# Second branch's keys and queries moved from the token-major stage into the quarter-product stage of a streaming-encoder kernel

## The chip, the cores and the metric

One core of one Trainium2 chip. The time is device microseconds of one launch. The engines are TensorE (PE, with its weight loads PEld), VectorE (DVE), ScalarE (ACT), GpSimd (POOL) and SyncE (SP), which issues most of the DMAs. Each engine works off its own list of instructions in the order of the program; they wait for each other through semaphores.

## The reference

One layer of a hybrid attention trunk, for 1024 prompt tokens and 64 sample tokens (1088 in all), width 1024. What the change touches is the projection of the second branch's queries and keys, and their norm over the 64 channels of each head:

```python
def rms_norm(x, w):
    xf = x.astype(jnp.float32)
    ms = jnp.mean(xf * xf, axis=-1, keepdims=True)
    return (xf * lax.rsqrt(ms + EPS)).astype(x.dtype) * w

def project(x, norm_w, w_in, q_norm_w, k_norm_w):
    h = rms_norm(x, norm_w) @ w_in                      # w_in: 1024 x 6144
    sb_q, sb_k, sb_v, sb_z, cb_q, cb_k, cb_v, cb_z, g_sb, g_cb = jnp.split(h, SPLIT_POINTS, axis=-1)
    ...
    cb_q = rms_norm(cb_q.reshape(lead + (N_HEADS_CB, HEAD_DIM)), q_norm_w)
    cb_k = rms_norm(cb_k.reshape(lead + (N_HEADS_CB, HEAD_DIM)), k_norm_w)
```

`cb_q` and `cb_k` are 512 columns each: 8 heads of 64. Behind them come two attentions (stick-breaking for the first branch, softmax over a band for the second), gates, projections and an output product. The last 512 prompt tokens and the sample tokens of `cb_k` are outputs too. All is float32.

## The kernel before

Every float32 operand of a product is split into a rounded high part and a low part (what rounding left), and a product is three matmuls: high by high, high by low, low by high.

**Token-major stage** (the block that begins at L198; product loop L450 to L537). The input is normed and transposed into `xhl` (channels on the partitions, 1088 tokens along the row). Then eight blocks of 256 columns of `w_in` (the list `NB`, L208) are multiplied, for 9 token tiles each, with tokens on the output's partitions: 8 channel blocks by 3 parts, 24 matmuls of 256 columns to a tile, 16 for the sample tile, 208 for a block. Two blocks are `sb_v`, two `cb_v`; the other four are `cb_k` (2560, 2816) and `cb_q` (2048, 2304). For these four, `evac_nat` copies the tile out and squares it on ACT, sums the squares of each head on DVE, and takes the power -1/2 on POOL (`rsqrt`, L247); `norm_nat` multiplies by it and by the weight on DVE one tile later; `post_nat` transposes the tile on PE (L349), splits it on ACT and DVE, and SP stores it. In the same loop SP loads the next weights, the caches are transposed (`cache_pair`), the bias table is written out (`make_rb`), and from the sixth block on `make_t` makes on DVE and ACT the sums of quarters of the input that the next stage needs (L502 to L515).

**Quarter-product stage** (L544 to L657). The list `pairs` (L145) names 12 pairs of 128-column blocks: keys and queries of the first branch (`k`, `q`), gates `silu` and `sig`. A pair is 256 columns by 1088 tokens, and is computed channel-major (columns of `w_in` on the output's partitions) by seven products of half the channels, 128 columns and half the tokens, with sums and differences of quarters as operands. A product `s` runs in two pieces (`XC`, L29) of 256 and 288 tokens with 12 matmuls each (L634), so a pair is 168 matmuls. Products 0, 1 and 2 open PSUM banks 1, 2 and 3; products 3, 4, 5 and 6 add to banks 1, 2, 2 and 3 (`BANK`, L614). ACT copies product 0 to `s1`; DVE adds after products 1, 4, 5 and 6; a finished quarter goes to `emit`: after product 3, product 4 (`u3`), product 5 (`s1`) and product 6 (`u2`), two pieces each. Product 5 adds to the bank that DVE reads after product 4, so it cannot start before that read.

`emit` applies the gate, or splits the quarter into high and low on ACT and DVE, and hands a store to a list (`soon`, L550) that `step` works off at the start of later products. Keys of the first branch are also transposed back on PE for their output (`out`, L590) through the two banks of `psF`. `prep` and `presum` make the operands of the product five and six places ahead: DVE sums quarters of weights (L401), ACT rounds them (L433), POOL takes the low parts (L434).

The order of all instructions is the order in which the Python code issues them; there is no planner. Behind this stage come the attention with the last projection units as filler (L782 to L1229) and the output product.

Of the kernel before, what the change touches and what calls it, by code (L numbers as in the profile page):

```python
# [8 lines left out]
F32 = mybir.dt.float32  # L9
# [23 lines left out]
def hybrid_step_kernel(ctx: ExitStack, tc: tile.TileContext, x_prompt, x_sample, c_sbk, c_sbv, c_cbk, c_cbv,  # L33
# [114 lines left out]
    for p in (0, 2):  # L148
        pairs += [("silu", 1536 + 128 * p, d_z["sb"][p:p + 2]), ("silu", 3584 + 128 * p, d_z["cb"][p:p + 2])]
# [48 lines left out]
    with ExitStack() as ph:  # L198
        sx = ExitStack()
        natx = sx.enter_context(tc.tile_pool(name="natx", bufs=2))  # L200
        pn = ph.enter_context(tc.tile_pool(name="pn", bufs=2, side="right"))
        p1x = ExitStack()
# [5 lines left out]
        NB = [1024, 2560, 2816, 2048, 2304, 1280, 3072, 3328]  # L208
        nb = len(NB)
        xts, xns, hl, cks = {}, {}, {}, {}  # L210
# [21 lines left out]
        wqk = pn.tile([128, 2, 64], F32, name="wqk", bufs=1)  # L232
# [3 lines left out]
        def load_rb():  # L236
            rbs[0] = p1.tile([128, 8, 257], F32, name="ck", bufs=1)
            SP.dma_start(rbs[0], rel_bias[0:1].to_broadcast([128, 8, 257]))

        def make_rb(h):  # L240
            rb = rbs[0]
            rx = p1.tile([128, 768], F32, name="rx", bufs=3)
# [53 lines left out]
        def evac_nat(i, t, ps):  # L296
# [6 lines left out]
            if grp in (2, 6):  # L303
                v = pn.tile([128, 256], F32, name="vst", bufs=3)
                A.activation(v[:r], ps[:r, :], AF.Copy)
                dst = d_sbv if grp == 2 else d_cbv
                SP.dma_start(dst[t * 128:t * 128 + r, n0:n0 + 256], v[:r])
                if grp == 2:
                    SP.dma_start(tok(o_sbv_p, o_sbv_s, t)[:, n0:n0 + 256], v[:r])
                elif t == 8:  # L310
                    SP.dma_start(o_cbv_s[:, n0:n0 + 256], v[:r])
                elif t >= 4:
                    SP.dma_start(o_cbv_p[(t - 4) * 128:(t - 3) * 128, n0:n0 + 256], v[:r])
                return
            sq = p1.tile([128, 256], F32, name="sqn")
            ms = p1.tile([128, 4], F32, name="msn")
            rs = p1.tile([128, 4], F32, name="rsn", bufs=3)
            qn = p1.tile([128, 4, 64], F32, name="qn", bufs=5)
            A.activation(qn[:r].rearrange("p h d -> p (h d)"), ps[:r, :], AF.Copy)
            A.activation(sq[:r], ps[:r, :], AF.Square)  # L320
            V.tensor_reduce(ms[:r], sq[:r].rearrange("p (h d) -> p h d", d=64), axis=AX.X, op=OP.add)
            rsqrt(rs[:r], ms[:r], 1.0 / 64, 4)
            return qn, rs

        def norm_nat(i, t, qn, rs):
            r = rows(t)
            n0 = NB[i] % 512
            isk = 1 if NB[i] // 512 == 5 else 0
            V.tensor_tensor(out=qn[:r], in0=qn[:r], in1=rs[:r, :, None].to_broadcast([r, 4, 64]), op=OP.mult)
            V.tensor_tensor(out=qn[:r], in0=qn[:r], in1=wqk[:r, None, isk, :].to_broadcast([r, 4, 64]),  # L330
                            op=OP.mult)
            if isk:
                if t == 8:
                    SP.dma_start(o_cbk_s[:, n0:n0 + 256], qn[:r].rearrange("p h d -> p (h d)"))
                elif t >= 4:
                    SP.dma_start(o_cbk_p[(t - 4) * 128:(t - 3) * 128, n0:n0 + 256],
                                 qn[:r].rearrange("p h d -> p (h d)"))

        def post_nat(i, t, qn):
            r = rows(t)  # L340
            c0 = NB[i]
            isk = 1 if c0 // 512 == 5 else 0
            p0 = (c0 % 512) // 128
            if t in (8, 4):
# [1176 lines left out]
```

## Time and profile before

| | us |
|---|---|
| median of 3 runs (lowest, highest) | 988.35 (987.6, 989.67) |
| the profiled execution's own time | 986.78 |
| its span | 985.0 |
| token-major products, from the first to the first quarter product | 227.5 from the start |
| quarter-product stage | 227.5 to 483.1 |
| PE busy | 962.0 |
| DVE, ACT, POOL busy | 630.1, 510.4, 346.2 |

The page of a profile gives busy times; the chain of work says which engine's instructions the end of the kernel hangs on; a table by groups of instructions gives the mean duration of one. A matmul's listed duration (278 ns for 256 columns) is its way through the array: the matmuls overlap, and the cost of one is the distance to the next, which the chain shows as a stretch of many. Idle time of an engine that is not the bottleneck costs nothing.

### The profile page before, as it was taken

What the parts mean: (1) busy time and instruction counts of PE and PEld (TensorE: products, weight loads), DVE (VectorE), ACT (ScalarE), POOL (GpSimd) and SP (SyncE); (2) the same over time, 40 slices, a digit from 0 to 9 for tenths busy, and PEclk for the clock granted to TensorE, in tenths of its full rate; (3) what the DMA queues carried; (4) which work ended last, traced back from release to release, by engine and by line L of the source; (5) the groups of instructions that cost most, each with busy time, mean ns of one, the idle gap of its engine ahead of it and who ended that gap; (6) DMA issues with size and microseconds to landing.
All of it is one profiled execution on the core that took longest, in us unless ns stands there. A gap on an engine that the chain in (4) does not pass through costs nothing.

```text
span 985.0 us, 20439 instructions
## 1 busy us (share of the span) xinstructions
PE 962.0 (98%) x7568; PEld 917.6 (93%) x7568; DVE 630.1 (64%) x1188; ACT 510.4 (52%) x1142; POOL 346.2 (35%) x356
## 2 busy tenths in 40 slices
PE   5999999999999999999999999999999999999998
PEld 5999999999999999999998888898888888999998
DVE  5456665696454655532239898997767765599735
ACT  5534443344443433433248787786876875466220
POOL 3376664115444554444211101101201101486641
PEclk9999999999999999999999999999999999999999
DMA  6727567533656333343298656666898772852642
GB/s 229 223 89 243 193 223 253 166 103 120 180 174 203 115 110 101 99 124 99 79 244 221 172 160 161 164 187 169 232 262 226 213 221 68 264 177 83 210 131 86
DMA packets 174243, 166.97 MB, mean 170 GB/s; under 512 B 34688, under 2 KB 160000, under 8 KB 174016
## 3 DMA queue, kind: packets, MB, share of 16 engines
q1 hardware_dynamic: 165424, 157.34, 53.7%
q10 hardware_dynamic: 8720, 8.33, 2.6%
q8 instruction: 60, 0.98, 0.4%
q14 instruction: 39, 0.32, 0.1%
HBM read 106.89 MB, written 58.72 MB: 168 GB/s over the span
## 4 chain that ended last, share of the span: by engine, by line
PE 90%; DMA 3%; ACT 3%; DVE 1%; SPq 1%; issue 1%; POOL 1%; DVEq 0%; ACTq 0%
PE b L634 25%; PE acc L464 19%; PE b L1435 8%; PE o L1127 7%; PE acc L782 7%; PE z L1033 6%; PE pt L1088 6%; PE b L924 5%; PE acc L882 3%; DMA wrawx<-in_w_in_dram 1%; PE pk L349 1%; ACT wT L1097 1%; PE pt L277 1%; SPq L51 1%; PE acc L1471 1%
## 5 line engine op out<-in xcount | busy, mean ns | idle before, releaser
L122 POOL TENSOR_TENSOR wlo<-wraw,whi 128x1024 fp32r<-128x1024 f32 x22 | 57.6, 2618 | 103.0 <-ACT whi L115 102.9
L1088 PE MATMUL pt<-ident,be 128*128 128x128 f32 (+1 forms) x568 | 87.2, 278 | 5.7 <-ACT wT L1097 1.9
L1056 DVE TENSOR_TENSOR_SCAN kp<-kp,imp 128x128 f32<-128x128 f32 (+7 forms) x64 | 88.3, 1379 | 0.6 <-ACT kp L1036 0.6
L1033 PE MATMUL z<-ks,sq 128*128 128x320 f32 (+5 forms) x384 | 83.2, 325 | 0.0
L1088 PEld LDWEIGHTS pt<-ident,be 128*128 128x128 f32 (+1 forms) x568 | 65.9, 140 | 16.8 <-issue 5.7
L1097 ACT ACTIVATE wT<-pt 128x512 f32<-128x512 f32 (+3 forms) x125 | 58.6, 501 | 39.0 <-PE pt L1088 38.9
L464 PE MATMUL acc<-whi,xa 128*128 128x256 f32 x256 | 74.2, 292 | 0.0
L464 PE MATMUL acc<-wlox,xm 128*128 128x256 f32 x256 | 70.8, 278 | 0.0
L464 PE MATMUL acc<-whi,xm 128*128 128x256 f32 x256 | 70.8, 278 | 0.0
L464 PE MATMUL acc<-wlo,xa 128*128 128x256 f32 x256 | 70.7, 278 | 0.0
L464 PE MATMUL acc<-whix,xb 128*128 128x256 f32 x256 | 70.7, 278 | 0.0
L464 PE MATMUL acc<-whix,xm 128*128 128x256 f32 x256 | 70.6, 278 | 0.0
L1033 PEld LDWEIGHTS z<-ks,sq 128*128 128x128 f32 x384 | 65.8, 188 | 1.1 <-issue 0.2
L1127 PE MATMUL o<-wT,vp 128*64 128x256 f32 (+1 forms) x608 | 66.7, 357 | 0.1
L782 PE MATMUL acc<-xm,whi 128*128 128x384 f32 (+1 forms) x192 | 65.2, 340 | 0.0
L1127 PEld LDWEIGHTS o<-wT,vp 128*64 128x64 f32 x608 | 42.3, 136 | 23.9 <-issue 5.7
L1057 DVE TENSOR_TENSOR be<-be,kp 128x128 f32<-128x128 f32 (+8 forms) x68 | 57.3, 843 | 9.4 <-ACT sg L757 0.5
L1036 ACT ACTIVATE kp<-z 128x384 f32<-128x384 f32 (+6 forms) x104 | 52.4, 504 | 9.5 <-PE z L1033 4.5
L642 DVE TENSOR_TENSOR u<-b,s 128x256 f32<-128x256 f32 (+1 forms) x48 | 20.8, 439 | 56.3 <-PE b L634 55.2
L1037 ACT ACTIVATE be<-z 128x384 f32<-128x384 f32 (+6 forms) x104 | 52.9, 508 | 0.0
L1060 ACT ACTIVATE be<-be,sm 128x640 f32<-128x640 f32 (+5 forms) x68 | 47.2, 694 | 9.5 <-DVE sm L1059 9.2
L1047 ACT ACTIVATE be<-be,sm 128x640 f32<-128x640 f32 (+5 forms) x68 | 47.2, 694 | 3.7 <-DVE sm L1039 3.4
(300 smaller groups left out, 3147.4 us busy)
## 6 DMA issues: line engine op xcount, KB each, us to landing
wraw<-in_w_in_dram SPq DMA_DIRECT2D x32, 512.0 KB, 4.6
wrawx<-in_w_in_dram SPq DMA_DIRECT2D x16, 512.0 KB, 4.5
sq<-d_qsbT SPq DMA_DIRECT2D x32, 192.0 KB, 3.6
sq<-d_qcbT SPq DMA_DIRECT2D x32, 192.0 KB, 4.4
xt<-in_x_prompt_dram SPq DMA_DIRECT2D x8, 512.0 KB, 5.8
d_kcbT<-hl SPq DMA_DIRECT2D x8, 512.0 KB, 4.4
d_qcbT<-hl SPq DMA_DIRECT2D x8, 512.0 KB, 5.7
d_ksbT<-hl SPq DMA_DIRECT2D x16, 256.0 KB, 2.5
```

The lines of the kernel that those rows point to most:

```text
L122: (eng or G).tensor_tensor(out=l, in0=raw, in1=h[:].bitcast(F32), op=OP.subtract)
L464: TE.matmul(ps, x, w, start=m == 0, stop=m == len(steps) - 1)
L634: TE.matmul(ps[:, :m], w[:, hl_, k], right[s](x)[:, k, a:b], start=s < 3 and k == 0 and e == 0, stop=k == 3 and e == 2, skip_group_check=s ...
L782: TE.matmul(ps[:, :b - a], w[:, k], xk(x, k)[:, a:b], start=k == 0 and n == 0, stop=k == KT - 1 and n == 2)
L1033: TE.matmul(z[:, :m], s[:, e, q0:q0 + 128], ks[:, h, o + x:o + y], start=e == parts[0][0], stop=e == parts[-1][0])
L1037: A.activation(be[:r, x:y], z[:r, :m], AF.Sigmoid, scale=0.125)
L1056: V.tensor_tensor_scan(kp[:r, n - 1::-1], kp[:r, n - 1::-1], im[:, ::-1], 0.0, op0=OP.mult, op1=OP.add)
L1057: V.tensor_tensor(out=be[:r, :n], in0=be[:r, :n], in1=kp[:r, 1:n + 1], op=OP.mult)
L1088: TE.transpose(pt[:kr, x, :r], be[:r, kb * 128:kb * 128 + kr], ident[:r, :r])
L1097: A.activation(w[:, sl:sl + m, q0:q0 + r], pt[:, :m, :r], AF.Copy)
L1127: TE.matmul(o[hd * 64:hd * 64 + 64, c0:c1], vv[:kr, kb, hd * 64:hd * 64 + 64], wT[b, p, j, hd, s // 4][:kr, s % 4, c0:c1] if j < 4 else wT ...
L1435: TE.matmul(ps[:, t], left[s](xs_, k)[:, ts_], wt_[:, k], start=s < 3 and t == k == e == 0, stop=k == 3 and e == 2, skip_group_check=s > 2 ...
```

## The change

The four `cb_k` and `cb_q` blocks leave the token-major stage (`NB` has four blocks left), and `norm_nat` and `post_nat` go. The list `pairs` gets two `ck` and two `cq` pairs, each set ahead of one of the four `silu` pairs, so there are 16 pairs. A `ck` or `cq` quarter goes to a new function, `normed`, in four steps that are spread over the following products, so that they run in the pair behind:

- `squares`, three products later: ACT squares the quarter and rounds the square, POOL takes the low part;
- `scale`, between the two pieces of the next product: PE multiplies both parts by `ones`, a block matrix with two 64 by 64 blocks of ones, so that each partition of the result holds the sum over its head; ACT takes the square root, DVE the reciprocal, both in place in a bank of `psF`; DVE multiplies the quarter by it and by the weight `wn`, in one instruction;
- `parts`, at the start of the product after: ACT and DVE split it, and SP stores it one product later;
- `k_out`, two products after `parts`, for the keys whose tokens are outputs: transposes back on PE.

Buffers change with it: `hl` has 8 instead of 4, `s1` and `u2` 4, `u3` 2, `ko` 3; the block of product 3 is one fixed tile (`w3`), and its second buffer holds the squares (`hold`). The bias table and caches move to other pools and earlier places, and `make_t` starts in the second block instead of the sixth.

```diff
@@ -146,7 +146,8 @@
     for p in (0, 2):
-        pairs += [("silu", 1536 + 128 * p, d_z["sb"][p:p + 2]), ("silu", 3584 + 128 * p, d_z["cb"][p:p + 2])]
+        pairs += [("ck", 2560 + 128 * p, p), ("silu", 1536 + 128 * p, d_z["sb"][p:p + 2]),
+                  ("cq", 2048 + 128 * p, p), ("silu", 3584 + 128 * p, d_z["cb"][p:p + 2])]
...
@@ -198,16 +199,22 @@
+        ones = natx.tile([128, 128], F32R, name="ones", bufs=1)
+        wn = natx.tile([128, 2], F32, name="wn", bufs=1)
...
-        NB = [1024, 2560, 2816, 2048, 2304, 1280, 3072, 3328]
+        NB = [1024, 1280, 3072, 3328]
...
+        for h in (slice(0, 64), slice(64, 128)):
+            G.memset(blk2[h, h], 1.0)
...
@@ -495,11 +455,17 @@
-                if (i, ti) == (4, 2):
+                if (i, ti) == (2, 6):
                     load_rb()
-                if 0 <= 9 * i + ti - 40 < 8:
-                    make_rb(9 * i + ti - 40)
-                if i >= 5 and p1x is not None and not pend and not raw1 and ti >= 3:
+                if 0 <= 9 * i + ti - 27 < 8:
+                    make_rb(9 * i + ti - 27)
...
+                if (i, ti) == (1, 1):
                     p1x.close()
...
-                    tw = [3]
+                    tw = [1]
...
@@ -574,10 +536,13 @@
+            p = arg + w
+            if kind in ("ck", "cq"):
+                normed(kind == "ck", p, half, c, n, src, ps)
+                return
...
+        def normed(isk, p, half, c, n, src, ps):
+
+            if ps:
+                kf = up.tile([128, 288], F32, name="kf", bufs=2)
+                V.tensor_copy(kf[:, :n], src[:, :n])
+                src = kf
+            x = src[:, :n]
+            dst = (d_kT if isk else d_qT)["cb"][p]
+
+            def squares():
+                sq = hold[:, 288 * nsq[0]:288 * nsq[0] + n]
+                nsq[0] = (nsq[0] + 1) % 3
+                h = up.tile([128, 2, 288], F32R, name="hl", bufs=HB)
+                A.activation(sq, x, AF.Square)
+                A.activation(h[:, 0, :n], sq, AF.Copy)
+                G.tensor_tensor(out=h[:, 1, :n], in0=sq, in1=h[:, 0, :n].bitcast(F32), op=OP.subtract)
+                mids.append([1, lambda: scale(h)])
+
+            def scale(h):
+                pt = psF.tile([128, 512], F32, name="acc")[:, :n]
+                for e in range(2):
+                    TE.matmul(pt, ones, h[:, e, :n], start=e == 0, stop=e == 1)
+                A.activation(pt, pt, AF.Sqrt, bias=eps64)
+                V.reciprocal(pt, pt)
+                V.scalar_tensor_tensor(x, x, wn[:, 1:2] if isk else wn[:, 0:1], pt, op0=OP.mult, op1=OP.mult)
+                soon(0, parts)
+
+            def parts():
+                h = up.tile([128, 2, 288], F32R, name="hl", bufs=HB)
+                A.activation(h[:, 0, :n], x, AF.Copy)
+                V.tensor_tensor(out=h[:, 1, :n], in0=x, in1=h[:, 0, :n].bitcast(F32), op=OP.subtract)
+                soon(0, lambda: stores(rdma, half, c, h[:, :, :n], dst[:]))
+                if isk and (half or c):
+                    soon(1, lambda: k_out(src, p, half, c, c * 256 if half else None, o_cbk_p, o_cbk_s))
+
+            soon(2, squares)
...
                     m = b - a
+                    if c:
+                        step(mids)
```

How the instructions stand. On DVE, before, in the first `silu` pair of the quarter-product stage (`u` and `s` are quarters, `b` a bank, `ws` a sum of weights, `hl` a result to store), from the adds after product 1 to the quarter after product 4:

```order
L642 TENSOR_TENSOR u_4507<-b_4494,s_4472 128x256
L642 TENSOR_TENSOR u_4522<-b_4509,s_4487 128x288
L401 TENSOR_TENSOR ws<-wraw,wrawx 128x512
L401 TENSOR_TENSOR ws<-ws,wraw 128x512
L574 TENSOR_TENSOR hl<-hl,b_4459 128x256
L574 TENSOR_TENSOR hl<-hl,b_4474 128x288
L642 TENSOR_TENSOR u_4608<-b_4494,s_4472 128x256
L642 TENSOR_TENSOR u_4622<-b_4509,s_4487 128x288
L654 TENSOR_TENSOR u_4608<-b_4531,u_4608 128x256
L574 TENSOR_TENSOR hl<-hl,u_4608 128x256
L654 TENSOR_TENSOR u_4622<-b_4544,u_4622 128x288
L574 TENSOR_TENSOR hl<-hl,u_4622 128x288
```

There a DVE instruction of the pair follows the PE product that feeds it, with weight sums in between. On DVE, after, in the first `silu` pair, which now follows a `ck` pair, from the first add after product 1 (L649 is the add that was L642, L363 the weight sum that was L401; `acc` is a bank of `psF`):

```order
L649 TENSOR_TENSOR u_3244<-b_3231,s_3183 128x256
L597 RECIPROCAL acc<-acc 128x256
L598 SCALAR_TENSOR_TENSOR u_3070<-u_3070,wn,acc 128x256
L597 RECIPROCAL acc<-acc 128x288
L598 SCALAR_TENSOR_TENSOR u_3084<-u_3084,wn,acc 128x288
L649 TENSOR_TENSOR u_3271<-b_3258,s_3210 128x288
L363 TENSOR_TENSOR ws<-wraw 128x512
L363 TENSOR_TENSOR ws<-ws,wraw 128x512
L604 TENSOR_TENSOR hl<-u_3070,hl 128x256
L604 TENSOR_TENSOR hl<-u_3084,hl 128x288
L597 RECIPROCAL acc<-acc 128x256
L598 SCALAR_TENSOR_TENSOR s_2939<-s_2939,wn,acc 128x256
```

The second add of product 1 now stands behind two reciprocals and two multiplications of the pair before. Further on in the same pair, on DVE, from the first gate (L536) to the first add after product 4 (L649):

```order
L536 TENSOR_TENSOR hl<-hl,b_3170 128x256
L597 RECIPROCAL acc<-acc 128x256
L598 SCALAR_TENSOR_TENSOR u_2974<-u_2974,wn,acc 128x256
L597 RECIPROCAL acc<-acc 128x288
L598 SCALAR_TENSOR_TENSOR u_2989<-u_2989,wn,acc 128x288
L536 TENSOR_TENSOR hl<-hl,b_3197 128x288
L604 TENSOR_TENSOR hl<-u_2974,hl 128x256
L604 TENSOR_TENSOR hl<-u_2989,hl 128x288
L649 TENSOR_TENSOR u_3437<-b_3231,s_3183 128x256
```

The add after product 4, which product 5 waits for, has the last group's reciprocals ahead of it. On ACT, before, in the first `silu` pair, around its first gate:

```order
L433 ACTIVATE wlo<-ws 128x512
L572 ACT_TABLE_LOAD
L572 ACTIVATE hl<-b_4459 128x256
L572 ACTIVATE hl<-b_4474 128x288
L433 ACTIVATE whix<-ws 128x512
L572 ACTIVATE hl<-u_4608 128x256
L572 ACTIVATE hl<-u_4622 128x288
```

One load of a function table stands there, and none in the pairs behind. On ACT, after, at the first gate of the first `silu` pair:

```order
L567 ACTIVATE kos<-acc 32x128
L603 ACTIVATE hl<-s_2939 128x256
L603 ACTIVATE hl<-s_2954 128x288
L534 ACT_TABLE_LOAD
L534 ACTIVATE hl<-b_3170 128x256
L596 ACT_TABLE_LOAD
L596 ACTIVATE acc<-acc,eps 128x256
L596 ACTIVATE acc<-acc,eps 128x288
L534 ACT_TABLE_LOAD
L534 ACTIVATE hl<-b_3197 128x288
```

Square roots (L596) and gates (L534) now alternate, with a table load at each turn. With the one ahead of the pair's first square root that is four to each `ck` or `cq` pair, 16 in the whole stage, where one stood before.

More of the change, by code (lines that the diff above doesn't have):

```diff
@@ L315, in evac_nat @@
[L315 to L337, printed above, removed]
@@ L588, in emit, with k_out @@
                 V.tensor_copy(kf[:, :n], src[:, :n])
-            def out():
-                pt = psF.tile([128, 512], F32, name="acc")
-                ko = up.tile([128, 2, 128], F32, name="ko", bufs=4)
-                cols = slice(p * 128, (p + 1) * 128)
+            soon(2 if (w, half) == (0, 1) else 1,
+                 lambda: k_out(kf, p, half, c, half * 512 + c * 256, o_sbk_p, o_sbk_s))
+        def k_out(kf, p, half, c, a, o_p, o_s):
+            pt = psF.tile([128, 512], F32, name="acc")
+            cols = slice(p * 128, (p + 1) * 128)
+            if a is not None:
```

148 lines of the change are left out of this document (64 added, 84 removed).

## The prediction

> **What bounds the kernel now.** I read the page first, then the quarter-product stage in the table by stretches, the chain, the waits of DVE in that stage, and last the durations by shape.
>
> ```profile
> span 985.0 us, 20439 instructions
> PE 962.0 (98%) x7568; PEld 917.6 (93%) x7568; DVE 630.1 (64%) x1188; ACT 510.4 (52%) x1142; POOL 346.2 (35%) x356
> ...
> 172.00:227.00 55.00, 55.00 (x487) 55.00 (x486) 46.47 (x62) 22.56 (x45) 8.76 (x4) 1.00 0.42 132
> 227.50:483.00 255.50, 255.50 (x2058) 254.63 (x2057) 119.20 (x232) 99.54 (x228) 121.42 (x84) 1.00 0.43 129
> ...
> DVE u L642 <- PE b L634: 55.2, 34, 6.8
> ```
>
> PE is busy for 98% of the span. The columns of the two stretches are length, then PE, PEld, DVE, ACT and POOL busy: in the whole quarter-product stage (the second) PE never stops, and DVE and ACT work less than half the time. The last row says who waits: DVE for PE, 55.2 us in 34 waits. So today work on DVE or ACT there costs nothing, and the time is the number of matmuls. The chain prices them:
>
> ```profile
> 168.94 0.22 PE pk L349 x2
> ...
> 172.21 55.33 PE acc L464 x488
> ...
> 256.39 0.44 PE acc L595 x4
> 256.82 0.11 PE acc L597
> ...
> 301.28 181.86 PE b L634 x1464
> ```
>
> A token-major matmul is 55.33/488 = 0.1134 us, a quarter-product matmul 181.86/1464 = 0.1242 us, a transpose 0.11 us.
>
> **PE's own work.** Removed: 4 blocks x 208 x 0.1134 = 94.3 us, and 72 transposes (4 blocks, 9 tiles, 2 each) x 0.11 = 7.9 us: -102.2 us. Added: 4 pairs x 168 x 0.1242 = 83.5 us; the products by ones, 32 quarters' pieces x 2 x 0.1242 = 7.9 us; key transposes, 6 for each of 4 column blocks x 0.11 = 2.6 us: +94.0 us. Net -8.2 us, all on the path, if nothing new makes PE wait.
>
> **What new work runs beside it.** Each `ck` or `cq` pair sends 8 pieces (4 quarters of 256 and 288 tokens) through `normed`, and nearly all of it falls into the first five products of the pair behind. The rows for it, DVE first:
>
> ```profile
> L1059 DVE RECIPROCAL sm<-sm 128x1 f32<-128x1 f32 x68 | 10.5, 154 | 1.9 <-ACT be L1047 1.9
> L537 DVE TENSOR_SCALAR wqk<-wqk 128x64 f32<-128x64 f32 x1 | 0.2, 178 | 0.0
> L244 DVE TENSOR_SCALAR rx<-ck 128x256 f32<-128x256 f32 x8 | 2.3, 283 | 0.0
> L1099 DVE COPY wT<-pt 128x512 f32<-128x512 f32 x21 | 14.5, 689 | 2.2 <-PE pt L1088 2.0
> L1099 DVE COPY wT<-pt 128x128 f32<-128x128 f32 x18 | 5.1, 284 | 0.3 <-PE pt L1088 0.3
> L642 DVE TENSOR_TENSOR u<-b,s 128x288 f32<-128x288 f32 x24 | 10.9, 455 | 20.7 <-PE b L634 20.6
> L642 DVE TENSOR_TENSOR u<-b,s 128x256 f32<-128x256 f32 x24 | 10.1, 422 | 35.6 <-PE b L634 34.6 <-ACT s L638 0.8
> L266 DVE SCALAR_TENSOR_TENSOR xn<-xt,rs,nw 128x512 f32<-128x512 f32 x16 | 11.3, 748 | 5.7 <-POOL rs L249 5.7
> L574 DVE TENSOR_TENSOR hl<-hl,u 128x288 f32<-128x288 f32 x8 | 3.7, 458 | 4.1 <-ACT hl L572 4.1
> L574 DVE TENSOR_TENSOR hl<-hl,u 128x256 f32<-128x256 f32 x8 | 3.4, 426 | 10.1 <-ACT hl L572 10.1
> L401 DVE TENSOR_TENSOR ws<-wraw,wrawx 128x512 f32<-128x512 f32 x4 | 4.2, 1062 | 0.0
> L401 DVE TENSOR_TENSOR ws<-ws,wraw 128x512 f32<-128x512 f32 x8 | 11.4, 1429 | 0.3
> ```
>
> *The reciprocal* decides the size. The trace has it for one column only. Were it like other work from a bank, it would cost what L642 does, 0.42 and 0.46 us: the lower end. But its 154 ns for one column is long: a TENSOR_SCALAR without columns is 178 - 64 x (283 - 178)/192 = 143 ns, a copy from a bank 284 - 128 x (689 - 284)/384 = 149 ns. So its one column takes 5 to 11 ns, where the copy's takes 1.05. I take 7.5 ns a column on 0.15 us, since the RECIPROCAL row is the operation itself: 2.07 us for 256 columns, 2.31 for 288. The upper end is 11 ns: 2.96 and 3.31 us. The Trainium skill, "VectorE: DVE Perf Modes", section "First, the fixed hardware budget", says the reciprocal is an iterated divide with a repeat count of 8. Eight of the copy's columns would be an estimated 8.4 ns, and the sum below about 8 us longer; one column of 5 to 11 ns agrees, but no run here shows a long one.
>
> ACT's rows, then POOL's and SP's:
>
> ```profile
> L572 ACT ACT_TABLE_LOAD x1 | 1.3, 1283 | 0.0
> ...
> L433 ACT ACTIVATE wlo<-ws 128x512 fp32r<-128x512 f32 x24 | 15.1, 630 | 33.3 <-DVE ws L401 30.7 <-PE b L634 2.3
> L572 ACT ACTIVATE hl<-u 128x288 f32<-128x288 f32 x16 | 7.1, 445 | 9.5 <-DVE u L649 5.8 <-DVE u L654 3.5
> L572 ACT ACTIVATE hl<-u 128x256 f32<-128x256 f32 x16 | 6.7, 418 | 35.4 <-DVE u L654 14.0 <-issue 8.6 <-DMA d_zsb<-hl 3.9
> L638 ACT ACTIVATE s<-b 128x288 f32<-128x288 f32 x12 | 4.8, 401 | 2.9 <-PE b L634 2.9
> L638 ACT ACTIVATE s<-b 128x256 f32<-128x256 f32 x12 | 4.4, 364 | 0.5 <-PE b L634 0.5
> ...
> L434 POOL TENSOR_TENSOR wlo<-ws,wlo 128x512 fp32r<-128x512 f32 x24 | 33.5, 1396 | 17.4 <-ACT wlo L433 12.3 <-PE acc L464 4.9
> L952 POOL TENSOR_TENSOR xb<-xm,xa 128x256 fp32r<-128x256 f32 x4 | 4.8, 1190 | 0.0
> ...
> 293.69 1.86 SPq L51 DMA_DIRECT2D d_ksbT<-hl x3
> ```
>
> ```profile
> 325.90 0.63 ACT L433 ACTIVATE wlo<-ws 128x512 fp32r<-128x512 f32 x1 [2.35 <-DVE ws L401]
> 326.55 1.28 ACT L572 ACT_TABLE_LOAD   x1
> 327.85 0.76 ACT L572 ACTIVATE hl<-b 128x256 f32<-128x256 f32 x2
> ```
>
> The one load of the stage stands 0.02 us behind the work ahead of it and as close to the work behind: it costs 1.28 us and no more. The Trainium skill, "ScalarE: Activation LUTs", section "What ACT_TABLE_LOAD costs", adds a drain of about 1.38 us to each switch. By that rule the three loads on the path of a window would cost about 4 us more, an estimated 17 us in all; the trace has no room for it here, so it is not in the sum.
>
> **One window.** It runs from the end of the first piece of product 0, behind a `ck` or `cq` pair, to the start of product 5. PE's own work in it is 4.5 products x 24 x 0.1242 = 13.4 us and 16 products by ones x 0.12 = 1.9 us: 15.3 us. `psF` has two banks, and DVE's multiplication frees one, so each group's products by ones wait for the group before; and product 5 waits for the add that stands on DVE behind the last group. So PE leaves the window when DVE is through:
>
> - start: copy of product 0 (0.36), table load (1.28), square root (taken like L638, 0.4): 2.1 us;
> - 8 reciprocals: 4 x 2.07 + 4 x 2.31 = 17.5 us;
> - 8 multiplications with two factors: L642 plus 0.06 (half of the way from an add's 512 columns, some 0.69, to L266's 0.748), 4 x 0.48 + 4 x 0.51 = 4.0 us;
> - 8 subtractions of `parts`: 4 x (0.43 + 0.46) = 3.5 us;
> - the pair's own: two adds 0.9, two gates 0.9, weight sums 1.06 + 1.43, the add that frees product 5 0.4: 4.7 us;
> - DVE waiting for ACT: a table load and the gate less the subtraction beside it, 1.28 + 0.4 - 0.45 = 1.2 us; a table load and the root less the gate's multiplication, 1.28 + 0.4 - 0.43 = 1.25 us; 0.1 us for three `parts`: 2.7 us.
>
> Sum 34.5 us, 19.2 more than PE's own 15.3. Four windows: +76.8 us. With the lower end of the reciprocal DVE's sum is 20.5 us, but then ACT decides (first rival); with the upper, 8 x 0.95 = 7.6 us more in each window, +30 us in all.
>
> Costed at nothing. POOL's 8 low parts (1.2 us each by L952) and some 5 of L434 are 16.6 us in a 34 us window. SP gets about 36 more issues in two pairs, 0.62 us each by the last row; the next weights stand ahead of them in its queue or have five products of lead. `make_t`'s 46.5 us of DVE (first stretch above) now run in the second and third block beside `cache_pair`; PE there waits for DVE only at a cache's bank, two tiles apart: 0 to 3 us. The norm's POOL powers that fall away were hidden, so they return nothing.
>
> **The sum.** 986.8 (the profiled execution; its span 985.0 and 1.8 around it) - 8.2 + 76.8 = 1055.4 us. The median before is 1.6 us above that execution, so 1057 us.
>
> **Rivals.**
> 1. *The reciprocal is cheap, and ACT is the bound.* Per window ACT has 4 table loads 5.1, 8 roots 3.1, two copies 0.8, four weight roundings 2.5, four squares and their roundings 3.45, 8 `parts` 3.45, two gates 0.8, key copies about 1: 20.2 us, and 1.5 of waiting for PE and DVE: 21.7, or 6.4 above PE's 15.3. 986.8 - 8.2 + 26 + 1.6 = 1006 us (998 to 1020). For it: nothing shows a long reciprocal. Against: its 154 ns.
> 2. *Faster.* If a window takes under 15.3 + 8.2/4 = 17.4 us, the fewer matmuls win; with all of it hidden, 988.4 - 8.2 = 980 us. For it: DVE and ACT are under half busy in the stage. Against: ACT's 20.2 us alone exceed 17.4, and the work stands together, in five products of 14.
> 3. *PE comes back slow after each wait.*
>
> ```profile
> 14.28 1.20 PE L464 MATMUL acc<-whix,xs 128*128 128x256 f32 x4
> 15.28 0.77 PE L464 MATMUL acc<-wlo,xs 128*128 128x256 f32 x4
> ...
> 19.38 0.63 PE L464 MATMUL acc<-whix,xm 128*128 128x256 f32 x4
> 19.85 0.63 PE L464 MATMUL acc<-whi,xm 128*128 128x256 f32 x4
> ```
>
> In the first work after the kernel's start four matmuls took 1.00 us, later 0.47, though the granted clock reads 1.00. If waits of 3 to 6 us bring that back, the stretch between two waits takes 6 instead of 3 us and still hides under DVE's 6 to 9; only after the last wait are some 2 to 4 us lost: 8 to 16 us in all, about 1069 us. Against it: waits shrink as the stretches grow. The Trainium skill, "TensorE: Matmul & The Clock Gate", section "What's actually happening", states such a gate, half the clock after an idle window of about 3.4 us; the start of this trace agrees in the factor of two.
>
> **How the numbers follow.** Within 0.2% is about what a measurement of this kernel cannot tell from no change. Forecast (reciprocal of 5 to 11 ns a column): 0.70, 1035 to 1083. PE slow as well: 0.08, 1060 to 1085. Cheap reciprocal: 0.16, 998 to 1020. Faster: 0.04; hidden but for a remainder that just eats the gain, same: 0.02. So slower 0.94. The range must reach into rival 1, from 1000 to 1083; the likeliest case's own is 1035 to 1083.
>
> **What would show it.** The profile after should have RECIPROCAL of 256 columns near 2.1 us, DVE busy nearly without a gap in four windows, PE waiting there for DVE (products by ones, product 5), some 75 us in all, 16 table loads in the stage, and the first quarter product near 125 us. Wrong is this if reciprocals take 0.5 us, if PE waits for ACT instead, or if token-major tiles wait for a cache's bank.

## The result, and the profile after

The changed kernel takes 1057.96 us (median of 4 runs, 1055.95 to 1061.83), the kernel before 988.25 us on the same chip: a ratio of 1.0708, 95% interval 1.0674 to 1.0742, so 7.1% slower. 1057 us was predicted. The profiled execution has a span of 1054.1 us.

From the page of the changed kernel, the span, the engines' busy time and the chain by engine:

```profile
span 1054.1 us, 20403 instructions
PE 977.9 (93%) x7424; PEld 928.5 (88%) x7424; DVE 681.0 (65%) x1201; ACT 560.1 (53%) x1218; POOL 329.4 (31%) x340
...
PE 75%; DVE 12%; ACT 5%; DMA 4%; issue 3%; SPq 1%; POOL 0%; DVEq 0%; ACTq 0%
```

PE has 144 matmuls fewer than before (7424 against 7568), yet its busy time rose from 962.0 to 977.9 us, and it is idle for 76 us where it was idle for 23. A quarter of the chain now belongs to others; half of that quarter is DVE's.

The table by stretches, in the quarter-product stage of the changed kernel. Each stretch is one pair of column blocks, from the first matmul of its product 0 to that of the next pair (length, then PE, PEld, DVE, ACT and POOL busy with the instructions in brackets, PEclk, DMA share, GB/s). The first is a `ck` pair itself; the other four are the pairs of sigmoids, each behind a `ck` or `cq` pair, in which that pair's norm runs:

```profile
224.61:245.51 20.90, 20.90 (x171) 20.90 (x170) 10.51 (x20) 9.37 (x22) 12.97 (x11) 1.00 0.48 148
245.51:285.89 40.38, 30.35 (x199) 28.84 (x198) 30.39 (x44) 22.84 (x49) 12.50 (x13) 0.87 0.27 82
306.78:345.98 39.20, 29.04 (x187) 27.93 (x185) 30.69 (x45) 21.81 (x44) 13.56 (x13) 0.87 0.28 85
366.83:408.38 41.55, 29.00 (x199) 26.91 (x198) 30.54 (x44) 22.72 (x49) 12.54 (x13) 0.92 0.26 80
429.23:466.83 37.60, 27.45 (x187) 26.34 (x186) 29.58 (x43) 20.96 (x43) 12.43 (x12) 0.91 0.24 74
```

A pair of PE's own work is 20.90 us. The four behind the norms together are 158.7 us; their own would be 4 x 20.90 + 7.9 for the products by ones + 2.6 for the key transposes = 94.1. So 64.6 us are lost there: 42.9 us in which PE is idle (158.7 less its 115.8 busy), and 21.7 us in which it is busy but slow; the granted clock is 0.87 to 0.92 on average over such a stretch.

The groups by shape of the changed kernel, for the work that came (busy, mean ns, idle before):

```profile
L597 DVE RECIPROCAL acc<-acc 128x288 f32<-128x288 f32 x16 | 31.3, 1959 | 0.0
L597 DVE RECIPROCAL acc<-acc 128x256 f32<-128x256 f32 x16 | 28.2, 1762 | 14.9 <-ACT acc L596 14.9
L589 POOL TENSOR_TENSOR hl<-wlox,hl 128x256 fp32r<-128x256 f32 x16 | 13.7, 855 | 0.0
L596 ACT ACT_TABLE_LOAD x8 | 10.3, 1283 | 0.1
L534 ACT ACT_TABLE_LOAD x8 | 10.3, 1283 | 0.1
L596 ACT ACTIVATE acc<-acc,eps 128x256 f32<-128x256 f32 x16 | 7.0, 438 | 0.1
...
L598 DVE SCALAR_TENSOR_TENSOR kf<-kf,wn,acc 128x256 f32<-128x256 f32 x4 | 1.9, 480 | 0.1
```

The chain of waits of the changed kernel through the second window, from the copy of product 0 to product 5 (start, length, what):

```profile
308.39 0.39 ACT s L645
308.80 1.28 ACT L596
310.09 0.46 ACT acc L596
310.57 1.78 DVE acc L597
312.37 0.48 DVE kf L598
...
328.71 1.28 ACT L534
...
330.41 0.86 ACT L596
...
332.18 1.78 DVE acc L597
...
337.96 0.35 DVE u L649
338.35 13.75 PE b L641 x96
```

For 30 us, from 308.4 to 338.35, the path runs through ACT and DVE alone. L596 without a tile is the load of the root's table, L534 that of the sigmoid's; with them the path holds eight reciprocals (the lines left out have the other six) and most of their multiplications.

What PE waits for in the changed kernel (total, times, longest; "..." stands for rows left out):

```profile
...
PE acc L595 <- DVE kf L598: 7.8, 4, 2.0
PE acc L563 <- DVE u L598: 7.5, 2, 4.1
PE b L641 <- DVE u L649: 6.7, 2, 3.4
PE acc L595 <- DVE s L598: 6.6, 5, 2.0
PE pc L333 <- DMA ck<-in_cache_cb_k_dram: 5.8, 1, 5.8
PE acc L563 <- ACT ko L571: 5.4, 4, 2.8
...
```

The first four shown are the norm: L595 and L563 want a bank of `psF` that a multiplication (L598) frees, L641 the bank that the add L649 frees. The last two had been costed at nothing: the second cache's transposes wait for its load, and key transposes wait for a copy to `ko`.

### The profile page after: what moved, and what is told of

It is laid out like the page before. It is cut to its first block, busy times and chain, and to the rows that moved or that the text cites. A ratio compares the mean times of both kernels' runs of the same rounds, so it can differ in the third digit from the quotient of the medians.

```text
span 1054.1 us, 20403 instructions
## 1 busy us (share of the span) xinstructions
PE 977.9 (93%) x7424; PEld 928.5 (88%) x7424; DVE 681.0 (65%) x1201; ACT 560.1 (53%) x1218; POOL 329.4 (31%) x340
## 4 chain that ended last, share of the span: by engine, by line
PE 75%; DVE 12%; ACT 5%; DMA 4%; issue 3%; SPq 1%; POOL 0%; DVEq 0%; ACTq 0%
PE b L641 27%; PE acc L789 8%; PE acc L428 8%; PE o L1134 6%; PE z L1040 6%; PE pt L1095 6%; PE b L1442 5%; DVE acc L597 5%; PE b L931 4%; PE acc L889 3%; ACT wT L1104 1%; DMA wrawx<-in_w_in_dram 1%; ACT L596 1%; DMA gt<-d_gsb 1%; PE pt L287 1%
## 5 line engine op out<-in xcount | busy, mean ns | idle before, releaser
L122 POOL TENSOR_TENSOR wlo<-wraw,whi 128x1024 fp32r<-128x1024 f32 x18 | 45.8, 2543 | 115.5 <-ACT whi L115 115.3
L649 DVE TENSOR_TENSOR u<-b,s 128x256 f32<-128x256 f32 x64 | 28.0, 440 | 81.2 <-PE b L641 65.0
L1104 ACT ACTIVATE wT<-pt 128x512 f32<-128x512 f32 (+3 forms) x125 | 58.5, 501 | 39.2 <-PE pt L1095 38.9
L398 POOL TENSOR_TENSOR whix<-ws,whix 128x512 fp32r<-128x512 f32 x32 | 42.1, 1314 | 90.5 <-ACT whix L397 90.5
L597 DVE RECIPROCAL acc<-acc 128x256 f32<-128x256 f32 (+1 forms) x32 | 59.5, 1860 | 14.9 <-ACT acc L596 14.9
L398 POOL TENSOR_TENSOR wlo<-ws,wlo 128x512 fp32r<-128x512 f32 x32 | 41.4, 1295 | 55.1 <-ACT wlo L397 55.1
L641 PE MATMUL b<-t3h,whi 128*128 128x256 f32 (+1 forms) x256 | 52.4, 294 | 6.7 <-DVE u L649 6.7
L641 PE MATMUL b<-t2h,whix 128*128 128x256 f32 (+1 forms) x256 | 55.9, 307 | 0.0
L641 PE MATMUL b<-t1h,wlo 128*128 128x256 f32 (+1 forms) x256 | 54.3, 299 | 0.0
L641 PE MATMUL b<-xm,wlox 128*128 128x256 f32 (+1 forms) x256 | 53.7, 296 | 0.0
L641 PE MATMUL b<-xa,whi 128*128 128x256 f32 (+1 forms) x256 | 52.9, 294 | 0.0
L1044 ACT ACTIVATE be<-z 128x384 f32<-128x384 f32 (+6 forms) x104 | 52.8, 508 | 0.0
```

The source lines that it names most:

```text
L398: G.tensor_tensor(out=t[:, 1], in0=src, in1=t[:, 0].bitcast(F32), op=OP.subtract)
L597: V.reciprocal(pt, pt)
L641: TE.matmul(ps[:, :m], w[:, hl_, k], right[s](x)[:, k, a:b], start=s < 3 and k == 0 and e == 0, stop=k == 3 and e == 2, skip_group_check=s ...
L1044: A.activation(be[:r, x:y], z[:r, :m], AF.Sigmoid, scale=0.125)
L1104: A.activation(w[:, sl:sl + m, q0:q0 + r], pt[:, :m, :r], AF.Copy)
```

## The experiments

The kernel before was run beside each group and took 987.4 to 988.6 us. "The four pairs" are the four stretches above: 158.7 us in the changed kernel, 94.1 of PE's own, each measured from the first matmuls in the trace. Differences in us are between medians.

**No reciprocal.**

```diff
-                V.reciprocal(pt, pt)
+                V.tensor_copy(pt, pt)
```

> The reciprocal is replaced by a copy of the same tile in place, so the norm is wrong but every wait and every instruction around it stays. Theory (DVE's reciprocals set the windows): each of the 8 in a window falls from 1.76 or 1.96 us to 0.42 or 0.46 us, 11.4 us per window; ACT's list of about 21.7 us then ends last, so a window falls from 30 to 33 us to about 22 us, and the time from 1058 to about 1020 us (1012 to 1028). Rival (the table loads on ACT set the windows): 1045 to 1058 us.

Measured: 1029.35 us, ratio 1.0413 (1.0387 to 1.0439), 28.6 us less; the four pairs take 132.6 us. By shape, the copies that stand in for the reciprocals in this run:

```profile
L597 DVE COPY acc<-acc 128x288 f32<-128x288 f32 x16 | 7.3, 458 | 0.0
L597 DVE COPY acc<-acc 128x256 f32<-128x256 f32 x16 | 6.8, 426 | 14.9 <-ACT acc L596 14.9
```

The 32 copies are 14.1 us where the reciprocals were 59.5, so DVE has 45.4 us less to do, and 26 to 29 of these come back. The reciprocal is on the path, but the time is 9 us above the one expected and just outside its range: something else takes over when it is gone.

**No change of tables.** The square root becomes a square, for which no table load appears in this run; it takes the same time (436 and 470 ns against 438 and 467).

```diff
-                A.activation(pt, pt, AF.Sqrt, bias=eps64)
+                A.activation(pt, pt, AF.Square, bias=eps64)
```

> The square root is replaced by a square with the same bias, which needs no other function table; the norm is wrong, the rest stays. All but one of the 16 table loads of the stage go. Theory (reciprocals): only the waits of DVE for ACT go, some 3.8 us per window, 15 us in all: 1043 us (1036 to 1050). Rival (table loads): most of the 63 us of the four windows goes, about 1000 us.

Measured: 1035.07 us, ratio 1.0478 (1.0457 to 1.05), 22.9 us less where 15 were expected; the four pairs 139.5 us, 19.2 less. One load is left in the stage, so 15 x 1.283 = 19.2 us of loads are gone: as much comes back as if every load had lain on the path in full. The chain above shows less, two loads of a window in full, a third by 0.86 us and not the fourth. So the size is measured, but that it is the fourth load which makes up the rest is not shown: in the second window of this run the path leaves DVE at 324.6, ahead of the fourth group, so more than the loads had become shorter there.

**Neither.** Both edits at once.

> Copy for the reciprocal and square for the square root together; the norm is wrong. Theory: DVE's list in a window is then about 15.7 us and ACT's about 15.1, PE's own 15.3, so the windows cost nearly nothing: 993 us (988 to 1003), still slower than the kernel before by the waits outside the windows (key pairs 7 us, cache load 6 us). Rival (spreading the norm over three engines costs by its hand-overs, whatever the durations): above 1010 us.

Measured: 1008.9 us, ratio 1.0201 (1.0173 to 1.0229), between the theory's range and the rival's bound; the four pairs 111.2 us. The two costs nearly add (28.6 and 22.9 alone, 49.1 together), but 17.1 us above PE's own remain, which neither a long reciprocal nor a table load can explain: in 12.1 of them PE is idle, the other 5.0 its own work takes longer. The chain of this run through the second window, a stretch of it:

```profile
301.05 0.31 ACT wlox L587
...
302.30 0.22 issue
302.52 0.75 ACT hl L603 x2
...
303.33 1.05 DVE hl L604
304.38 0.33 DVE u L649
304.72 0.35 DVE acc L597
```

ACT's squares (L587), the `parts` (L603 and L604), the add and DVE's copies (L597) follow one another: short pieces of ACT and DVE, with some 0.25 us of issue between some of them, and PE waits for the last. Read from the chain, that is a remainder of hand-overs; no run takes them away.

**No norm at all.** `ck` and `cq` are split into two parts and stored like `k` and `q`; squares, products by ones, root, reciprocal and multiplication are left out.

```diff
-            if kind in ("ck", "cq"):
-                normed(kind == "ck", p, half, c, n, src, ps)
-                return
```

> The ck and cq quarters are split and stored as the first branch's are, with no norm at all; the products, stores and key outputs stay. This is the price of the move alone. Theory: 988.4 - 102.2 + 83.5 + 2.6 = 972 us for PE's work, plus the waits outside the windows that the trace shows (7 in the key pairs, 4 in the token-major stage, 2 behind): 985 us (978 to 992). Rival (the gain in matmuls is real and nothing outside the windows was lost): 972 us.

Measured: 984.29 us, ratio 0.9966 (0.995 to 0.9982). The move of the products alone makes the kernel a little faster, by 3.7 us where PE's sum says 16.1 (without the products by ones). Most of the missing 12 are stalls in places that were costed at nothing, which the next run and the last one take up.

**Buffers.** A second `kos` (the kernel before had two, the change has one), and the second cache's transposes one tile later.

```diff
-                if i in (1, 2) and ti in (0, 2, 4, 6):
-                    cache_pair("sb" if i == 1 else "cb", ti // 2)
+                if (i, ti) in ((1, 0), (1, 2), (1, 4), (1, 6)):
+                    cache_pair("sb", ti // 2)
+                if (i, ti) in ((2, 2), (2, 4), (2, 6), (2, 8)):
+                    cache_pair("cb", ti // 2 - 1)
...
-                kos = up.tile([32, 128], F32, name="kos", bufs=1)
+                kos = up.tile([32, 128], F32, name="kos", bufs=2)
```

> A second buffer for kos (the 32 rows of keys that ACT copies and SP stores) and the second cache's four transposes one tile later, with the rows of the bias tables moved behind them; nothing else. Theory: the two stalls that the prediction had put at nothing, some 7 us in the key pairs (ACT waits for the store of kos) and the 5.8 us in which PE waits for the second cache's load, go: 1046 us (1043 to 1050). Rival: PE meets another wait at the same places, the load is late whatever stands there: 1053 or more.

Measured: 1051.67 us, ratio 1.0647 (1.0624 to 1.067): 6.3 us less where 12 were expected. The wait for the cache fell from 5.8 to 0.3 us, and the first quarter product comes at 124.7 instead of 129.5 us. The four pairs of the first branch's keys and queries fell only from 95.1 to 93.2 us (88.7 before the change): the single `kos` was not their only cause. In the changed kernel ACT waits there for the store of `kos`, 4.9 us in two waits; in this run it waits for the store of a `ko` instead, 3.4 us in three, and `ko` has three buffers where there were four. Kernels whose code is the same up to there took 91.9 to 95.3 us for these four pairs, so part of the excess differs from one execution to the next.

**Spread out.** The third group's squares one product later, the fourth's two.

```diff
-            soon(2, squares)
+            soon({(0, 0): 2, (1, 1): 2, (1, 0): 3, (0, 1): 4}[w, half], squares)
```

> The same norm, its four groups of pieces spread out: the squares of the third group (w 1, half 0) one product later, those of the fourth (w 0, half 1) two products later than now. Theory: the windows lose time because 32 us of dependent work of ACT and DVE stand in front of 15.3 us of PE; with two more products (12 us of PE) in front of the last group each window loses some 10 us less, four of them 40: 1018 us (1008 to 1032). Rival: it is not the room but the serial way of each group through sqrt, reciprocal and product behind its table loads, and a sqrt that now falls between the sigmoids of the next pair adds table loads (up to 8, 1.28 us each): 1050 or more.

Measured: 1060.86 us, ratio 1.0717 (1.0681 to 1.0752): nothing gained; the rival held. By shape, and from PE's waits, in this run:

```profile
L596 ACT ACT_TABLE_LOAD x12 | 15.4, 1283 | 0.2
L534 ACT ACT_TABLE_LOAD x12 | 15.4, 1283 | 0.2
```

```profile
PE b L641 <- DVE u L649: 10.2, 2, 5.1
PE acc L565 <- DVE u L598: 10.2, 2, 5.1
```

24 table loads instead of 16, since later roots fall between the sigmoids; and behind `ck` pairs the key transposes (L565) now meet the late multiplications. Behind `cq` pairs the two pairs shrank from 39.2 and 37.6 to 35.9 and 36.0 us, behind `ck` they grew from 40.4 and 41.5 to 44.4 and 44.6.

**Spread, with another order of the pairs and the buffers.** As the last two, and:

```diff
+    for p in (0, 2):
+        pairs += [("ck", 2560 + 128 * p, p), ("k", 512 + 128 * p, p),
+                  ("cq", 2048 + 128 * p, p), ("q", 128 * p, p)]
     for p in (0, 2):
-        pairs += [("ck", 2560 + 128 * p, p), ("silu", 1536 + 128 * p, d_z["sb"][p:p + 2]),
-                  ("cq", 2048 + 128 * p, p), ("silu", 3584 + 128 * p, d_z["cb"][p:p + 2])]
+        pairs += [("silu", 1536 + 128 * p, d_z["sb"][p:p + 2]), ("silu", 3584 + 128 * p, d_z["cb"][p:p + 2])]
```

> The spread of e6, the buffers of e5, and the order of the pairs changed so that a pair of the first branch's keys or queries, not a pair of sigmoids, follows each pair of the second branch (sqrt and sigmoid no longer alternate: 5 or so table loads in place of 16). Theory: all three costs go and what is left is PE's own work, 8.2 us under before, plus 1.6 in the tail and a few hand-overs: 987 us (980 to 997). Rival: the first branch's pairs bring two-part copies of their own (ACT and DVE some 1 us each for a piece), which take the place of the sigmoids in the windows: 1005 or more.

Measured: 1029.89 us, ratio 1.0429 (1.041 to 1.0449): the rival's side. Two table loads are left in the stage. 28 us come back, which is what the table loads (20 to 23) and the buffers (6.3) were worth by themselves; spreading the groups added nothing that can be told. The pairs behind a norm still take 44.3, 31.3, 44.6 and 28.8 us.

**The reciprocal twice.** A second one in place behind each.

> Each reciprocal is followed by another in place (32 more, 1.76 and 1.96 us long), so the norm is not the norm. Theory: the reciprocals lie on the path of the windows with all but a few per cent of their time, taking them away gave 26 to 29 us for 45 us that a copy saves; so 59.5 us more of them cost all of it, 50 to 60: 1112 us (1105 to 1118). Rival: about half of each is covered by PE or ACT as it is now: 1090 or less.

Measured: 1110.74 us, ratio 1.1253 (1.1223 to 1.1282), 52.8 us more; the four pairs 218.0 us, 59.3 more, for 59.5 us of reciprocals (the first branch's four pairs took 92.2 us in this run, 3 less). The table by stretches, the first two of the four pairs:

```profile
242.19:296.02 53.83, 33.58 (x198) 31.40 (x197) 45.29 (x52) 23.09 (x49) 12.53 (x13) 0.75 0.20 61
316.87:372.31 55.44, 33.88 (x186) 32.68 (x185) 45.84 (x53) 22.18 (x44) 13.68 (x13) 0.75 0.22 68
```

By the chain the second window, from the copy of product 0 to product 5, grew from 30.0 to 45.2 us (318.48 to 363.64), by 15.2 for 14.9 us of reciprocals, and so did the fourth; the two behind `ck` pairs grew by 13.3 and 11.9. The granted clock falls to 0.75 and less, and PE's busy time grows by 3 to 7 us a pair; nearly all of that hides, since the pairs grow by no more than the reciprocals' time.

**The root into SBUF.** A bank of `psF` is free once ACT has read it, not after the reciprocal and the multiplication.

```diff
-                A.activation(pt, pt, AF.Sqrt, bias=eps64)
-                V.reciprocal(pt, pt)
-                V.scalar_tensor_tensor(x, x, wn[:, 1:2] if isk else wn[:, 0:1], pt, op0=OP.mult, op1=OP.mult)
+                r = up.tile([128, 2, 288], F32R, name="hl", bufs=HB)[:, 0, :n].bitcast(F32)
+                A.activation(r, pt, AF.Sqrt, bias=eps64)
+                V.reciprocal(r, r)
+                V.scalar_tensor_tensor(x, x, wn[:, 1:2] if isk else wn[:, 0:1], r, op0=OP.mult, op1=OP.mult)
```

> One change in the norm: ACT writes the square root from PSUM to a tile in SBUF, and the reciprocal and the product read it there, so that a bank of the ring of two is free after the sqrt (0.46 us) and not after reciprocal and product (2.3 us more a piece). Theory: PE, which computes in order, waits in the windows for that ring; DVE was busy 22.5 of 28.0 us of the first window, so up to 5.5 us of each goes, and four of them give 1036 us (1030 to 1046). Rival: the windows are DVE's sum, the banks only show where PE happens to stand: 1053 or more.

Measured: 1054.99 us, ratio 1.0666 (1.0649 to 1.0684), an interval that overlaps that of the changed kernel; the four pairs 157.8 us. The rival held: the banks only show where PE happens to stand. The first of PE's waits in this run:

```profile
PE b L642 <- DVE u L650: 21.1, 4, 10.7
...
```

The wait for the multiplication is gone; in its place PE waits 26.2 us for the root on ACT, and the wait for DVE's add has grown from 6.7 to 21.1 us. PE gets further and then waits for the same queue. The reciprocal from SBUF takes 1.75 and 1.94 us, like the one from the bank.

**All together.** The root into SBUF, the buffers, the pairs in the order `ck`, `q`, `cq`, `k`, the groups two products apart, and the norm's key transposes one product earlier:

```diff
-            soon(2, squares)
+            soon({(1, 1): 1, (0, 0): 4, (1, 0): 4, (0, 1): 5}[w, half], squares)
```

> The square root to SBUF of e9, the buffers of e5, a pair of queries or keys of the first branch behind each pair of the second (queries behind keys, keys behind queries, so that not both have keys to transpose), and the four groups of each norm two products apart (squares one product behind the end of the second group, then three, five and seven products behind the pair's end by turns), so that some 23 us of DVE's work for a norm lie beside 42 us of PE. Theory: all of the window's loss but PE's 2 us of products by ones goes: 984 us (977 to 994), at or under before. Rival: DVE's queue still holds up a sum on which a bank of PE's products waits, group by group: 1005 or more.

Measured: 1033.76 us, ratio 1.0455 (1.0439 to 1.0471). Far from the 984 of the theory, on the rival's side. The table by stretches of this run, the pair behind the last norm and the one behind that:

```profile
320.09:357.06 36.97, 30.33 (x202) 28.82 (x200) 30.46 (x44) 18.11 (x47) 13.78 (x13) 0.82 0.37 113
357.06:378.55 21.49, 21.49 (x176) 21.48 (x174) 13.07 (x23) 9.98 (x24) 8.83 (x6) 1.00 0.55 160
```

PE's waits of this run:

```profile
PE b L644 <- DVE u L652: 11.3, 4, 3.3
...
PE acc L597 <- ACT kos L569: 7.3, 2, 3.6
...
```

The theory had set 23 us of the norm's DVE work against 42 us of PE, and left out two things. The groups, two products of 3.0 us apart, still lie nearly all in the one pair behind; and that pair has DVE work of its own: 30.46 us of DVE against about 24.9 of PE (20.90, and 2.0 each for the products by ones and the key transposes). Both pairs together have 30.46 + 13.07 = 43.5 us of DVE against about 46 of PE's own. So hiding the norm would need DVE busy almost without a gap, and a PE that never waits for a queue in which a group of two pieces stands for 4.7 us (1.76 + 0.48 + 1.96 + 0.52) in one go. That is an account of the trace; no run tests it alone.

**All together, with four `ko`.** As the last, with four buffers for `ko` and seven for `hl`.

> As e10, with four buffers for ko in place of three, as before the change, and seven for hl in place of eight. Theory: the key pairs of the first branch, which were 2 us a pair longer than before the change, wait for the store of a ko; 4 to 8 us less than e10. Rival: seven hl are too few once a norm is spread and each root takes one: 5 us or more above e10.

Measured: 1035.11 us, ratio 1.0469 (1.0445 to 1.0492). Neither theory's number: no difference that can be told.

**The move alone, with the buffers of before.** No norm at all, the second cache's transposes one tile later, four `ko`, two `kos`, four `hl`.

> The move of the products alone, in its best case: the second branch's pairs stored with no norm at all, as in the run without the norm, the second cache's transposes one tile later, and the buffers as they were before the change (four ko, two kos, four hl). Theory: without the norm and without the stalls the move is worth PE's own sum, 102.2 us that go against 83.5 and 2.6 that come, so 16.1 less, and the tail 1.6 more: 974 us (971 to 978) where before stands near 988; the stalls that were put at nothing had hidden some 10 us of it. Rival: the key pairs' longer last product is not the buffers but the order of their transposes and stores, and the load stays late: 980 or more.

Measured: 973.54 us, ratio 0.986 (0.9836 to 0.9884), 13.8 us faster than before. The longest of PE's waits in this run, and the only one left in the quarter-product stage:

```profile
PE pt L287 <- DVE xn L276: 8.6, 2, 7.5
...
PE acc L564 <- DVE kf L553: 1.0, 2, 0.7
```

The move is worth nearly PE's own 16.1 us. The first branch's four pairs take 90.2 us, 1.5 above before; with the buffers of the change they took 91.9 without the norm as well. So the change has a gain of 14 us in it, and the norm that comes with it costs 84 (1057.96 - 973.54), some 11 of them through the buffers and the place of the cache's transposes (984.29 - 973.54).

## Why the prediction was right, and where its terms were off

The time (1057 against 1057.96) is nearer than the steps, and that near it is luck: the steps miss by 12 us both ways. Against the trace, in us:

| step | predicted | measured |
|---|---|---|
| work before the quarter products | -102.2 | -97.9 (first quarter product at 129.5, before at 227.4) |
| the first branch's four pairs | 0 | +6.5 (95.1 against 88.7) |
| the four new pairs' products | +83.5 | +83.6 (4 x 20.90) |
| the four pairs behind them: windows, ones, key transposes | +87.3 | +75.1 (158.7 - 83.6) |
| the stages behind | 0 | +1.8 (the span is 69.1 longer, the rows above sum to 67.3) |

**PE's own work** came as priced: a new pair is 20.90 us, and the run of the move alone shows 13.8 of its 16.1 us.

**The window** was right as a mechanism: PE leaves it when DVE is through. Two runs show that, not only the chain. With DVE's reciprocals doubled the four pairs grow by all of it (59.3 of 59.5 us), and with the banks freed early they stay (157.8 against 158.7). The window measured 30.0 us in the chain above, 34.5 was the forecast; the other three took 30.0 to 33.3.

**The reciprocal's size** was the term that was off: 1.762 and 1.959 us, not 2.07 and 2.31. That is 4 x 0.31 + 4 x 0.35 = 2.6 us a window and 10.5 us in all, most of the 12 us by which the windows came out shorter. The two weight sums were off too, 0.68 + 0.69 us in each window where 1.06 + 1.43 were priced, 4.5 us in all; slow matmuls took 3.6 us of this back, as told below. Between the two shapes it is (1959 - 1762)/32 = 6.2 ns a column, inside the 5 to 11 that the single column allowed, on 0.19 us. The Trainium skill, "VectorE: DVE Perf Modes", section "First, the fixed hardware budget", gives the reciprocal a repeat count of 8, which was an estimated 8.4 ns; the measurement decides for less. The other rows were near: the multiplication 0.48 and 0.51 us as forecast (half of the way from 0.69 to 0.748 is 0.03 us, not the 0.06 that was added, but the size fits), POOL's low parts 0.86 us under their bound of 1.19.

**The table loads** were worth more than priced: 16 loads as forecast, 1.283 us each without a gap, of which I had put three in each window on the path, 15.4 us in all. The runs without them gave back 19.2 us in the four pairs, and 21.4 where the reciprocals were copies (22.9 and 20.5 in the medians); what the rest is stays open. The rule with a drain of 1.38 us in the Trainium skill, "ScalarE: Activation LUTs", section "What ACT_TABLE_LOAD costs", finds no room: the loads stand 0.02 us from their neighbours in the chain, and 15 of them gave back 19.2 us, their own time.

**What was costed at nothing** cost 12 us. `make_t` beside `cache_pair` had "0 to 3 us": the first of the second cache's transposes waited 5.8 us for its load, which landed at 78.86. The single buffer had not held it up, for the last transposes that read it ended at 65.8. The trace has this instead:

```profile
71.29 0.68 DVE L336 TENSOR_TENSOR hc<-pc,hc 128x512 fp32r<-128x512 f32 x1
72.00 0.32 SPq L51 DMA_DIRECT2D d_csbT<-hc  x1
72.41 0.39 SPq L327 DMA_DIRECT2D ck<-in_cache_cb_k_dram  x1
```

SP issues the load behind the store of the last `hc`, that store waits for DVE's subtraction (L336), and the subtraction stands behind the sums of `make_t`. So `make_t` did cost PE something, but through SP's queue and not at a cache's bank. The run with the transposes one tile later got 4.7 back. The first branch's key pairs were not looked at: they and the query pairs took 95.1 us, 90.2 with the buffers of before in the move alone, and 91.9 to 95.3 with fewer `ko` and `kos`; why this differs between executions stays open. These misses and the shorter windows have opposite signs, and that is why the sum fits.

**"PE waits for DVE some 75 us in all"** was wrong in form. Idle are 42.9 us in the four pairs, the other 21.7 are slow matmuls. Behind the last wait of the first and of the third window the chain has this:

```profile
274.71 4.53 PE b L641 x24
...
279.35 3.01 PE b L641 x24
...
396.63 5.04 PE b L641 x24
```

A product of 24 matmuls took 4.53 and 5.04 us, where the next took 3.01. In the second window the product behind the last wait and the one after it stand in the table by stretches so:

```profile
338.35:343.00 4.65, 4.65 (x25) 4.65 (x26) 3.01 (x8) 1.80 (x4) 1.55 (x1) 0.64 0.07 17
343.00:345.98 2.98, 2.98 (x26) 2.98 (x25) 1.94 (x5) 1.38 (x3) 1.20 (x2) 1.00 0.90 283
```

With a granted clock of 0.64 the product took 4.65 us, with 1.00 it took 2.98. So the third rival's mechanism exists, below the price of 8 to 16 us that it had: on the chain it is 1.5 us in the first window, 2.1 in the third and 1.8 behind the second (13.75 us for the 96 matmuls of the chain above against 96 x 0.1242), and next to nothing behind the fourth, some 5 us in all. The other slow matmuls hide under DVE's time, as the rival's text had allowed. The Trainium skill, "TensorE: Matmul & The Clock Gate", section "What's actually happening", has the clock halved after an idle window of about 3.4 us. The trace agrees in direction: the waits ahead of these three products were 3.39, 4.14 and 3.37 us long. Matmuls also came slow behind two waits of 1.15 and 1.95 us close together.

**The first rival** (a cheap reciprocal, 1006 us) can be read off the run with the copies: 1029. Its window was priced well for the pairs behind `cq`, 21.7 us against 22.5 in that run's chain; the windows behind `ck` took 25.0 and 26.0. The four pairs lose 38.5 us there (132.6 - 94.1) where it had 26, and the same 12 us that were costed at nothing come on top. **The second** (faster) needs windows under 17.4 us: even with neither long reciprocals nor table loads the four pairs are 17.1 us above PE's own, twice the 8.2 us that the fewer matmuls give.

What stays open: whether an order of the norm's steps exists that hides all of it. Four tries did not find one; the best, 1030 us, is 28 under the changed kernel and 42 above the one before. By the stretches of the run with all together DVE would have to be busy nearly all the time for it.

## What to carry to other kernels

"PE never stops and DVE is half idle" does not mean that DVE can take half as much again: PE runs in order, so what counts is how much dependent DVE and ACT work stands between two of its products, in the one window where it stands. Price such a window as the sum of the queue that frees the banks, with every table load in it and every hand-over, and test it by doubling its longest instruction: if the time grows by the whole of it, the queue is the bound, and freeing banks or moving steps by a product or two will not help. And look at the buffers and places that a change gives up to make room: here they took 11 of the 14 us that the move had to win. A load that had room of its own can come late because of a store that stands ahead of it in SP's queue.

## What was not expected of the hardware

A fp32 reciprocal of 128 x 256 took 1.76 us, four times a copy of the same shape (0.43), and as long from SBUF as from PSUM. A wait of PE does not only cost its length: in the four pairs the granted clock fell to 0.87 to 0.92, with twice the reciprocals to 0.71 to 0.75, and 22 to 42 us more of PE's time were spent on the same matmuls (115.8 and 136.5 against 94.1). In the changed kernel only some 5 of the 22 us lengthened the run, since DVE was the later one for the rest.
